# A one-core encoder layer on Trainium2: weight stores on another queue, an index row in its own buffer, merged one-hots, 48 leading u tiles

## The chip, the cores and the metric

The kernel runs on one core of a Trainium2 chip. The metric is the device time of one execution in microseconds; three executions of a kernel are timed and their median is given. A separate execution is recorded by the hardware profiler; its own time stands beside its span.

## The reference, cut to what matters

One layer on 512 tokens of width 1024 (16 meta tokens stand in front until the second half). The first half is an attention part: an input projection, differential attention and a gated linear attention in two directions, and an output projection onto the residual stream. The second half is a product-key retrieval, and it is what the change touches:

```python
q = (xi @ w_q).reshape(n, 8, 2, 128)                      # 8 heads, 2 sub-keys
s = einsum('nhpc,hpkc->nhpk', q, sub_keys)                # 128 scores each
ts, ti = top_k(s, 16)
cand_s = ts[:, :, 0, :, None] + ts[:, :, 1, None, :]      # 16 x 16 candidates
cand_i = ti[:, :, 0, :, None] * 128 + ti[:, :, 1, None, :]
best_s, best_p = top_k(cand_s, 16)
idx  = take_along_axis(cand_i, best_p)                    # 128 experts a token
gate = softmax(best_s)
act  = gelu(einsum('nd,nhkd->nhk', xi, u[idx]))
out  = einsum('nhk,nhkd->nd', gate * act, v[idx])
```

There are 128 x 128 experts, each with one row of `u` and one of `v`, 1024 wide. The sum is added to the residual stream and a last RMSNorm gives the output.

## The kernel before, in words

Tokens are taken in four tiles of 128. For tile 0 the chosen rows are gathered: 128 indirect DMAs fetch rows of `u`, VectorE makes a dot product of each with the token (L265), and 128 more fetch rows of `v`, which VectorE adds up (L263). For tiles 1 to 3, 384 tokens, the layer is computed densely: all `u` rows times all tokens, Gelu, times a matrix W of gates that is zero except at the chosen experts, times all `v` rows. All matmuls that need fp32 accuracy split each operand into a high and a low part and use three products (`mm3`, L126).

The run has these stages, with their stretches in the profile:

- 0 to about 466 us: the attention part, the projection, the 16 score units (`q` and `keys`, L919 to L940) and the searches for the 16 largest (`top16`, L182). The scores wait in a ring `sc` of SC = 16 buffers, in a pool `qs` that is closed when the searches are done.
- About 466 to 846, the middle. It interleaves two things. The u tiles, LA = 60 of them ahead of the v stage (`u_tile`, L1044): SP loads 512 KB into a ring of two buffers (`raw`, L108), ScalarE casts the high part (L114), GpSimd subtracts the low part (L116, `lo`), TensorE does 24 matmuls (L127 to L129), ScalarE applies Gelu (L1055) and stores the result to DRAM (`A_d`, L1057). And the weight building, `wbuild` (L961): the rest of the top-k (`topk2`, L189), then for each of 48 blocks of 8 tokens two one-hot tensors (L993), their products with the high and low part of the gate (L996, L994; in every fourth block ScalarE makes the high product, L999), 16 matmuls (L1021, L1022), and two copies into a staging tile (L1024). Every fourth block fills a staging tile of 2 MB, and SP stores it to DRAM (`W_d`, L1026). Four buffers hold one-hots. The first block of a token tile needs the transposed selections `sel` (L974).
- From about 846: the v stage, 128 v tiles of 18 matmuls (L1080 to L1084). It reads W and the stored activations back (L1111, L1113); the u tiles that are not leading run here, from v tile LA on, with their low part on VectorE instead of GpSimd.

How fast the building goes is set in the main loop: after u tile i, `wbuild` is advanced until the share of its cost reaches (i + 1)/(LA-ET-1), with ET = 6. The gathers are pulled by the same loops: RA a tile in the middle (from tile 12 on, L1137), RV a tile in the v stage before tile LA, RUV a tile after it (L1154). A gather is followed by its dot product when more than LAG = 3 are pending; what is left is done at the start of the v stage (`v_init`). The top-k's last tile `eq` and the gathered rows share a ring of four buffers.

The program order is not the order on the engines: a planner simulates the timeline and sets each engine's order by it. Once set, every engine and every DMA queue runs its own list in order.

SP issues all loads and the `W_d` stores from one queue; ScalarE issues the `A_d` stores. The index row 0 to 127, `iof`, is loaded by SP (L949) into a pool `wk` that takes the memory of `qs`, and VectorE spreads it into `ioh` (L950), the pattern that the one-hots compare with.

Of the kernel before, what the change touches and what calls it, by code (L numbers as in the profile page):

```python
# [9 lines left out]
F32 = mybir.dt.float32  # L10
F32R = mybir.dt.float32r
F16 = mybir.dt.float16
# [34 lines left out]
C1 = 3.0  # L47
WB = 4
WL = 1
SC = 16  # L50
TK = 1, 1, 1, 1
RB = 2
PT = {'gemm': 'g', 'half': 'g', 'meta': 'p', 'fin': 'p', 'gate': 'p', 'pair': 'a', 'kn': 'a', 'state': 'a', 'go': 'a', 'wo': 'g', 'hs': 'a', 'nat': 'a'}
# [6 lines left out]
VS = 4  # L60
VR = 5
VG = 6
RA = 0.4
RV = 0.85
RUV = 2.85
LA = 60
NCAND = 80
TCA = {'schedule_with_timeline_sim': True}
ORDER = 'GGGxGGGGGGGkGGggvgqggukugguqugguuukuvgqgukqgwuwuuuwwwuuuww'
# [13 lines left out]
def _emit(ctx, tc, I, out):  # L83
# [69 lines left out]
    hrs = cst.tile([P, NT], F32, name="hrs")  # L153
    hrow = cst.tile([P, T], F32, name="hrow")
    io16 = cst.tile([P, TOPK], F32, name="io16")

    def half(name, tag, j, n):
        return big.tile([P, KD // 2, n], F32R, name=f"{name}{j}", tag=f"{tag}{j}")
# [20 lines left out]
    def fx(name, shape, tag, dt=F32):  # L179
        return f1.tile(list(shape), dt, name=name, tag=tag)  # L180
# [8 lines left out]
    def topk2(a, b, sm, cand, tf, eq, zs):  # L189
        ts_ = tsv[:, b, 2 * a:2 * a + 2].rearrange("p t h c r -> p (t h) c r")  # L190
        ti_ = tiv[:, b, 2 * a:2 * a + 2].rearrange("p t h c r -> p (t h) c r")
        nc.vector.tensor_copy(tf, ti_)
        nc.vector.tensor_add(cand[:, :, 0:16], ts_[:, :, 1, :], ts_[:, :, 0, 0:1].to_broadcast([P, PH, 16]))
        nc.vector.tensor_add(cand[:, :, 16:72].rearrange("p h (a b) -> p h a b", b=8),
                             ts_[:, :, 1, None, 0:8].to_broadcast([P, PH, 7, 8]),
                             ts_[:, :, 0, 1:8, None].to_broadcast([P, PH, 7, 8]))
        nc.vector.tensor_add(cand[:, :, 72:80], ts_[:, :, 0, 8:16], ts_[:, :, 1, 0:1].to_broadcast([P, PH, 8]))
        bsv = sm("bsv")
        bp = sm("bp", U32)
        for h in range(PH):  # L200
            top16(bsv[:, h, :], bp[:, h, :], cand[:, h, :])
            if h % 4 == 3:
                yield
        gate = sm("gate")
        nc.vector.tensor_sub(gate, bsv, bsv[:, :, 0:1].to_broadcast([P, PH, TOPK]))
        g4 = gate.rearrange("p (t h) r -> p t (h r)", h=4)
        nc.vector.tensor_mul(g4, g4, hrs[:, 2 * a:2 * a + 2, None].to_broadcast([P, 2, 4 * TOPK]))
        def th(v):
            return v.rearrange("p (t h) r -> p t h r", h=4)

        def dst(j):
            return sel[:, j, 2 * a:2 * a + 2, 4 * b:4 * b + 4, :]

        row = sm("row", U32)
        nc.vector.tensor_scalar(row, bp, 3, None, op0=ALU.logical_shift_right)
        nc.vector.tensor_scalar(bp, bp, 7, None, op0=ALU.bitwise_and)
        rf = sm("rf")
        cf = sm("cf")
        nc.vector.tensor_copy(rf, row)
        nc.vector.tensor_copy(cf, bp)  # L220
        t9 = sm("t9")
        nc.vector.scalar_tensor_tensor(t9, rf, 9.0, cf, op0=ALU.is_equal, op1=ALU.mult)
        t1 = sm("bsv")
        nc.vector.tensor_scalar(t1, rf, 1.0, 8.0, op0=ALU.is_equal, op1=ALU.mult)
        nc.vector.tensor_add(cf, cf, t1)
        nc.vector.tensor_sub(cf, cf, t9)
        nc.vector.tensor_scalar(rf, rf, -1.0, 0.0, op0=ALU.add, op1=ALU.max)
        nc.vector.tensor_add(rf, rf, t9)
        yield
        for j, pos in enumerate((rf, cf)):  # L230
            nc.vector.tensor_tensor(eq, pos[:, :, :, None].to_broadcast([P, PH, TOPK, TOPK]),
                                    io16[:, None, None, :].to_broadcast([P, PH, TOPK, TOPK]), op=ALU.is_equal)
            nc.vector.tensor_mul(eq, eq, tf[:, :, j, None, :].to_broadcast([P, PH, TOPK, TOPK]))
            nc.vector.tensor_add(eq[:, :, :, :8], eq[:, :, :, :8], eq[:, :, :, 8:])
            nc.vector.tensor_add(eq[:, :, :, :4], eq[:, :, :, :4], eq[:, :, :, 4:8])
            nc.vector.tensor_add(eq[:, :, :, :2], eq[:, :, :, :2], eq[:, :, :, 2:4])
            nc.vector.tensor_add(dst(1 + j), th(eq[:, :, :, 0]), th(eq[:, :, :, 1]))
            if j == 0:
                yield
        nc.scalar.activation(gate, gate, AF.Exp)  # L240
        nc.vector.tensor_reduce(zs, gate, axis=AX.X, op=ALU.add)
        nc.vector.reciprocal(zs, zs)
        nc.vector.tensor_mul(dst(0), th(gate), th(zs[:, :, None].to_broadcast([P, PH, TOPK])))
        yield
# [114 lines left out]

    nc.sync.dma_start(out=ln2, in_=I["ln2"])  # L360
    nc.sync.dma_start(out=io16, in_=I["iota"][:, :TOPK].to_broadcast([P, TOPK]))
    ropc = fx("ropc", [P, TM], "ropc")
    nc.sync.dma_start(out=ropc, in_=I["ropc"])
    rops = fx("rops", [P, TM], "rops")
# [528 lines left out]
    qst = ExitStack()  # L893
    qs = qst.enter_context(tc.tile_pool(name="qs", bufs=1))

    keys = qs.tile([P, 2 * PH, NK], F32, name="keys")
    nc.sync.dma_start(out=keys, in_=I["keys"])

# [46 lines left out]
    wk = mid.enter_context(tc.tile_pool(name="wk", bufs=1))  # L945
    wk2 = mid.enter_context(tc.tile_pool(name="wk2", bufs=2))
    ioh = wk.tile([P, NK, QI], F16, name="ioh")
    iof = wk.tile([P, NK], F32, name="iof")
    nc.sync.dma_start(out=iof, in_=I["iota"].to_broadcast([P, NK]))  # L949
    nc.vector.tensor_copy(ioh, iof[:, :, None].to_broadcast([P, NK, QI]))  # L950
    sp = sparse()
    def residual(c2):
# [8 lines left out]
    def wbuild():  # L961
# [8 lines left out]
        def prep(t, m0):  # L970
            if m0 == 0:
# [2 lines left out]
                    nc.tensor.transpose(out=tr[:, j, :], in_=sel[:, j, t].rearrange("p h r -> p (h r)"), identity=ident)  # L974
                gT = wk2.tile([P, P], F32, name="gT")
                nc.scalar.activation(gT, tr[:, 0, :], AF.Copy, scale=GS)
                iT = wk2.tile([P, 2, P], F16, name="iT")
                nc.scalar.copy(iT, tr[:, 1:3, :])
                gh = wk2.tile([P, P], F16, name="gh")
                nc.vector.tensor_copy(gh, gT)  # L980
                gl = wk2.tile([P, P], F16, name="gl")
                nc.vector.tensor_sub(gl, gT, gh)
                cur[t] = gT, iT, gh, gl
            gT, iT, gh, gl = cur[t]
            sh = [P, OB // QI, NK, QI]

            def tok(v):
                return v[:, m0:m0 + OB].rearrange("p (g q) -> p g q", q=QI)[:, :, None, :].to_broadcast(sh)

            oh = big.tile([P, 4] + sh[1:], F16, name="oh", tag=("hi0", "hi1", "lo0", "lo1")[(t * P + m0) // OB % WB])  # L990
            o12, ol, od = oh[:, :2], oh[:, 2], oh[:, 3]
            for j in range(2):
                nc.vector.tensor_tensor(o12[:, j], tok(iT[:, j]), ioh[:, None, :, :].to_broadcast(sh), op=ALU.is_equal)  # L993
            nc.vector.tensor_mul(ol, o12[:, 0], tok(gl))  # L994
            if m0 // OB % DM < DN:
                nc.vector.tensor_mul(od, o12[:, 0], tok(gh))  # L996
            else:
                for m in range(OB):
                    nc.scalar.activation(od[:, m // QI, :, m % QI], o12[:, 0, m // QI, :, m % QI], AF.Copy,  # L999
                                         scale=gT[:, m0 + m:m0 + m + 1])  # L1000
# [4 lines left out]
        for n, (t, m0) in enumerate(steps):  # L1005
# [17 lines left out]
                qq = q0 + 4 * g_  # L1023
                nc.scalar.activation(stg[:, :, qq:qq + 4].rearrange("p i n -> p n i"), b, AF.Copy, scale=1.0 / GS)  # L1024
            if q0 + OB == BL:
                nc.sync.dma_start(out=W_d[:, ((t - 1) * P + m0) // BL], in_=stg)  # L1026
            yield 2.2

    U, V = {}, {}
# [238 lines left out]
```

## Time and profile before

| | before |
|---|---|
| median of three runs | 1678.32 us (1671.53 to 1680.73) |
| the profiled execution | 1682.47 us, span 1680.7 us |
| TensorE busy | 1574.4 us (94%) |
| VectorE busy | 1291.4 us (77%) |
| ScalarE busy | 739.6 us (44%) |
| GpSimd busy | 677.1 us (40%) |
| mean granted TensorE clock | 0.973 |
| moved by DMA | 387.42 MB |

The span runs from the first to the last instruction of the profiled execution. In the rows PE is TensorE, PEld its weight load, DVE VectorE, ACT ScalarE, POOL GpSimd and SP SyncE; a q behind an engine's name is its queue of DMA issues. L12 is line 12 of the kernel before. [...]

### The profile page before, as it was taken

How to read it: one execution, taken by the hardware profiler on the slowest of the kernel's cores; microseconds unless marked ns; L12 is line 12 of the kernel's file. 1: busy time of each engine (PE TensorE's matmuls, PEld its weight loads, DVE VectorE, ACT ScalarE, POOL GpSimd, SP SyncE). 2: the span in 40 equal slices, each digit the busy share in tenths (PEclk: the TensorE clock that was granted, in tenths of full speed). 3: DMA queues.
4: the chain of work that ended last, by engine and by line, in shares of the span. 5: the costliest groups of instructions: out<-in, count | busy, mean ns of one | idle time of the engine just before them, and what ended most of it. 6: DMA issues, size and time to landing. Idle time of an engine off the chain costs nothing.

```text
span 1680.7 us, 24243 instructions
## 1 busy us (share of the span) xinstructions
PE 1574.4 (94%) x8793; PEld 1392.4 (83%) x8793; DVE 1291.4 (77%) x2529; ACT 739.6 (44%) x1229; POOL 677.1 (40%) x465
## 2 busy tenths in 40 slices
PE   6999998989986789979989999999999999999998
PEld 6888886768876689878978888889999999988996
DVE  3888768647999998948247777778887888778777
ACT  5454555543324474867533333333333333333334
POOL 3443112076334467475411212154545444344442
PEclk9999999989997989999999999999999999999999
DMA  6112222232224557656999999899999998999885
GB/s 232 54 46 81 69 61 69 84 118 89 78 73 149 176 193 250 239 218 252 328 366 342 326 314 326 278 313 389 321 329 326 336 327 315 319 339 327 308 276 185
DMA packets 152360, 387.42 MB, mean 231 GB/s; under 512 B 12752, under 2 KB 71376, under 8 KB 150576
## 3 DMA queue, kind: packets, MB, share of 16 engines
q1 hardware_dynamic: 106160, 238.79, 41.2%
q0 software_dynamic: 36864, 134.23, 22.8%
q10 hardware_dynamic: 9216, 12.85, 2.1%
q8 instruction: 69, 1.13, 0.3%
q14 instruction: 51, 0.42, 0.1%
HBM read 342.56 MB, written 40.63 MB: 228 GB/s over the span
## 4 chain that ended last, share of the span: by engine, by line
PE 28%; issue 18%; DVE 12%; POOL 10%; DMA 6%; ACT 3%; SPq 1%; POOLq 0%; ACTq 0%; DVEq 0%
POOL gat L251 7%; PE banka L1080 4%; PE banka L1083 4%; PE banka L1084 4%; POOL lo L116 3%; PE bankp L1080 2%; PE bankp L1083 2%; PE bankp L1084 2%; PE bankg L129 2%; DMA gat<-v,idx 2%; PE bankg L127 2%; PE bankg L128 2%; DMA raw<-uT 2%; DVE oh L993 2%; DMA gat<-u,idx 1%
## 5 line engine op out<-in xcount | busy, mean ns | idle before, releaser
L116 POOL TENSOR_TENSOR lo<-raw,hi 128x1024 fp32r<-128x1024 f32 x81 | 238.4, 2947 | 228.8 <-ACT hi L114 220.4
L114 ACT CAST hi<-raw 128x1024 fp32r<-128x1024 f32 x177 | 185.8, 1051 | 289.6 <-PE bankg L128 159.1
L127 PE MATMUL bankg<-un_hi,hi 128*128 128x384 f32 x880 | 300.1, 341 | 12.2 <-ACT act L1055 12.2
L129 PE MATMUL bankg<-un_hi,lo 128*128 128x384 f32 x880 | 299.6, 341 | 5.3 <-POOL lo L116 5.2
L128 PE MATMUL bankg<-un_lo,hi 128*128 128x384 f32 x880 | 297.9, 338 | 0.0
L251 POOL DMA_INDIRECT gat<-u,idx x128 | 157.8, 1232 | 299.5 <-PE bankp L1084 252.1
L251 POOL DMA_INDIRECT gat<-v,idx x128 | 167.8, 1311 | 207.6 <-PE bankp L1084 180.4
L263 DVE SCALAR_TENSOR_TENSOR acc<-gat,sact,acc 128x1024 f32<-128x1024 f32 x128 | 164.2, 1283 | 72.2 <-DMA gat<-v,idx 61.6
L265 DVE CUSTOM_DVE_ANT_0 gat<-gat,hn 128x1024 f32<-128x1024 f32 x128 | 162.9, 1282 | 53.2 <-DMA gat<-u,idx 53.1
L127 PEld LDWEIGHTS bankg<-un_hi,hi 128*128 128x128 f32 x880 | 168.1, 191 | 16.1 <-ACT act L1055 12.5
L135 DVE TENSOR_TENSOR vhl<-vraw,vhl 128x1024 fp32r<-128x1024 f32 x128 | 157.1, 1228 | 30.9 <-ACT vhl L134 30.8
L129 PEld LDWEIGHTS bankg<-un_hi,lo 128*128 128x128 f32 x880 | 167.9, 191 | 8.1 <-POOL lo L116 6.8
L128 PEld LDWEIGHTS bankg<-un_lo,hi 128*128 128x128 f32 x880 | 167.7, 191 | 3.4
L134 ACT CAST vhl<-vraw 128x1024 fp32r<-128x1024 f32 x128 | 134.2, 1049 | 46.3 <-PE bankp L1084 33.4
L116 DVE TENSOR_TENSOR lo<-raw,hi 128x1024 fp32r<-128x1024 f32 x96 | 117.8, 1228 | 24.2 <-ACT hi L114 23.0
L1024 ACT ACTIVATE stg<-banka 128x512 f32<-128x512 f32 x96 | 96.2, 1140 | 1.7 <-PE banka L1022 0.9
L993 DVE TENSOR_TENSOR oh<-iT,ioh 128x1024 f16<-128x1024 f16 x96 | 80.8, 888 | 2.4 <-PE banka L1022 2.4
L1021 PE MATMUL banka<-oh 128*128 128x128 f16 x384 | 55.3, 233 | 22.1 <-DVE oh L996 12.7
L1055 ACT ACTIVATE act<-bankg 128x384 f32<-128x384 f32 x110 | 53.4, 486 | 23.2 <-PE bankg L129 12.1
L1021 PEld LDWEIGHTS <-oh 128*128 128x128 f16 x384 | 39.2, 104 | 20.8 <-DVE oh L996 15.0
L1022 PE MATMUL banka<-oh 128*128 128x128 f16 x384 | 54.3, 233 | 0.7 <-DVE oh L994 0.7
L129 PE MATMUL bankp<-un_hi,lo 128*128 128x384 f32 x144 | 48.7, 338 | 4.5 <-POOL lo L116 4.5
(2283 smaller groups left out, 3906.3 us busy)
## 6 DMA issues: line engine op xcount, KB each, us to landing
raw<-uT SPq DMA_DIRECT2D x128, 512.0 KB
vraw<-v SPq DMA_DIRECT2D x128, 512.0 KB
W_d<-stg SPq DMA_DIRECT2D x12, 2048.0 KB
wa<-W_d SPq DMA_DIRECT2D x32, 768.0 KB
A_d<-act ACTq DMA_DIRECT2D x60, 192.0 KB
wa<-A_d SPq DMA_DIRECT2D x15, 768.0 KB
raw<-wq SPq DMA_DIRECT2D x16, 512.0 KB
raw<-win_n SPq DMA_DIRECT2D x12, 512.0 KB
```

What stands on the lines that cost most here:

```text
L114: nc.scalar.copy(hi, raw)
L116: (eng or nc.vector).tensor_sub(lo, raw, hi.bitcast(F32))
L127: nc.tensor.matmul(o, lhsT=ah, rhs=bh, start=start, stop=False)
L128: nc.tensor.matmul(o, lhsT=ah, rhs=bl, start=False, stop=False)
L129: return nc.tensor.matmul(o, lhsT=al, rhs=bh, start=False, stop=stop)
L134: last[0] = nc.scalar.copy(hi, src).ins.name
L135: (eng or nc.vector).tensor_sub(lo, src, hi.bitcast(F32))
L251: g = nc.gpsimd.indirect_dma_start(out=r, out_offset=None, in_=src, in_offset=bass.IndirectOffsetOnAxis(ap=idx[:, hk:hk + 1], axis=0))
L263: nc.vector.scalar_tensor_tensor(acc0, r, sact[:, hk:hk + 1], acc0, op0=ALU.mult, op1=ALU.add)
L265: nc.vector.tensor_tensor_reduce(r, r, hn0, scale=1.0, scalar=0.0, op0=ALU.mult, op1=ALU.add, accum_out=sact[:, hk:hk + 1])
L993: nc.vector.tensor_tensor(o12[:, j], tok(iT[:, j]), ioh[:, None, :, :].to_broadcast(sh), op=ALU.is_equal)
L1080: m0 = nc.tensor.matmul(o, lhsT=gh_[:, tc_], rhs=vh[:, dc], start=(j == 0), stop=False, skip_group_check=True)
```

## The change

- `W_d` stores are issued by ScalarE instead of SP.
- `iof` moves to the pool `w1`, which stays open to the end, and its load is issued ahead of that of `keys`; SC goes from 16 to 15.
- The two one-hots of a block are made by one compare of 2048 elements instead of two of 1024, and the two products by one multiplication where VectorE makes both. For that the transposed indices `iT` and the two gate parts `gs` are laid out block by block, and the four parts of `oh` lie one after another.
- LA goes from 60 to 48; RA from 0.4 to 0.15; RUV from 2.85 to 2.7.
- The positions in the top-k are written as bf16 (`rb`, `cb`), and compared with a bf16 index row (`io16b`, one small copy at the start) instead of in fp32.

```diff
-SC = 16
+SC = 15
-RA = 0.4
+RA = 0.15
-RUV = 2.85
-LA = 60
+RUV = 2.7
+LA = 48
+    io16b = cst.tile([P, TOPK], BF, name="io16b")
+        rb = sm("rb", BF)
+        cb = sm("cb", BF)
-        nc.vector.tensor_sub(cf, cf, t9)
+        nc.vector.tensor_sub(cb, cf, t9)
-        nc.vector.tensor_add(rf, rf, t9)
+        nc.vector.tensor_add(rb, rf, t9)
-        for j, pos in enumerate((rf, cf)):
+        for j, pos in enumerate((rb, cb)):
-                                    io16[:, None, None, :].to_broadcast([P, PH, TOPK, TOPK]), op=ALU.is_equal)
+                                    io16b[:, None, None, :].to_broadcast([P, PH, TOPK, TOPK]), op=ALU.is_equal)
+    nc.vector.tensor_copy(io16b, io16)
+    iof = w1.tile([P, NK], F32, name="iof")
+    nc.sync.dma_start(out=iof, in_=I["iota"].to_broadcast([P, NK]))
     keys = qs.tile([P, 2 * PH, NK], F32, name="keys")
...
-    iof = wk.tile([P, NK], F32, name="iof")
-    nc.sync.dma_start(out=iof, in_=I["iota"].to_broadcast([P, NK]))
     nc.vector.tensor_copy(ioh, iof[:, :, None].to_broadcast([P, NK, QI]))
...
-                iT = wk2.tile([P, 2, P], F16, name="iT")
-                nc.scalar.copy(iT, tr[:, 1:3, :])
-                gh = wk2.tile([P, P], F16, name="gh")
-                nc.vector.tensor_copy(gh, gT)
-                gl = wk2.tile([P, P], F16, name="gl")
-                nc.vector.tensor_sub(gl, gT, gh)
+                iT = wk2.tile([P, P // OB, 2, OB], F16, name="iT")
+                nc.scalar.copy(iT.rearrange("p b j m -> p j b m"), tr[:, 1:3, :].rearrange("p j (b m) -> p j b m", m=OB))
+                gs = wk2.tile([P, P // OB, 2, OB], F16, name="gs")
+                g8 = gT.rearrange("p (b m) -> p b m", m=OB)
+                nc.vector.tensor_copy(gs[:, :, 0, :], g8)
+                nc.vector.tensor_sub(gs[:, :, 1, :], g8, gs[:, :, 0, :])
...
-            for j in range(2):
-                nc.vector.tensor_tensor(o12[:, j], tok(iT[:, j]), ioh[:, None, :, :].to_broadcast(sh), op=ALU.is_equal)
-            nc.vector.tensor_mul(ol, o12[:, 0], tok(gl))
-            if m0 // OB % DM < DN:
-                nc.vector.tensor_mul(od, o12[:, 0], tok(gh))
+            nc.vector.tensor_tensor(o12, tok(iT[:, blk].rearrange("p j m -> p (j m)")),
+                                    ioh[:, None, :, :].to_broadcast([P, 2 * GQ, NK, QI]), op=ALU.is_equal)
+            o12 = o12.rearrange("p (j g) k q -> p j g k q", j=2)
+            od, ol = oh[:, 2 * GQ:3 * GQ], oh[:, 3 * GQ:]
+            if blk % DM < DN:
+                nc.vector.tensor_mul(oh[:, 2 * GQ:].rearrange("p (c g) k q -> p c (g k q)", c=2).rearrange("p c (g k q) -> p c g k q", k=NK, q=QI),
+                                     o12[:, None, 0].to_broadcast([P, 2] + sh[1:]),
+                                     gs[:, blk].rearrange("p c (g q) -> p c g q", q=QI)[:, :, :, None, :].to_broadcast([P, 2] + sh[1:]))
             else:
+                nc.vector.tensor_mul(ol, o12[:, 0], tok(gs[:, blk, 1]))
...
-                nc.sync.dma_start(out=W_d[:, ((t - 1) * P + m0) // BL], in_=stg)
+                nc.scalar.dma_start(out=W_d[:, ((t - 1) * P + m0) // BL], in_=stg)
```

## Rows read from the trace of the kernel before

**Rows 1.** The stage table: busy time of each engine in five stretches, in us (with its count of instructions), then the granted clock of TensorE as a share of 2.4 GHz, the busy share of the DMA engines and GB/s.

```profile
0.00:466.00 466.00, 435.03 (x2584) 362.34 (x2584) 336.15 (x1027) 225.87 (x476) 168.81 (x151) 0.97 0.28 90
466.00:560.00 94.00, 67.64 (x358) 65.33 (x357) 91.64 (x430) 32.26 (x44) 36.58 (x16) 0.84 0.33 109
560.00:820.00 260.00, 228.44 (x1737) 218.52 (x1736) 209.32 (x239) 175.97 (x277) 157.06 (x55) 0.95 0.65 234
846.00:1092.00 246.00, 245.82 (x1094) 205.30 (x1095) 180.63 (x261) 90.25 (x126) 45.97 (x46) 0.99 0.94 324
1092.00:1640.00 548.00, 545.72 (x2760) 493.86 (x2759) 439.81 (x521) 191.56 (x262) 251.10 (x188) 1.00 0.92 325
```

**Rows 2.** TensorE's waits in the stretch 466 to 560 us: who waited for whom, us in total, times, longest.

```profile
PE bankg L127 <- ACT act L1055: 12.2, 1, 12.2
PE bankp L974 <- DVE sel L237: 8.0, 2, 5.5
PE bankp L974 <- DVE sel L243: 5.1, 1, 5.1
```

**Rows 3.** TensorE's waits in the stretch 560 to 820 us, same columns.

```profile
PE banka L1021 <- DVE oh L996: 12.7, 9, 3.4
PE banka L1021 <- ACT stg L1024: 9.3, 9, 3.7
PE bankp L129 <- POOL lo L116: 4.5, 1, 4.5
PE bankg L129 <- POOL lo L116: 4.2, 2, 3.9
```

**Rows 4.** ScalarE's groups by line in the stretch 560 to 820 us: count, then busy us and mean ns of one, then idle us ahead of them and what ended it.

```profile
L114 ACT CAST hi<-raw 128x1024 fp32r<-128x1024 f32 x40 | 42.2, 1055 | 45.2 <-DMA raw<-uT 34.6 <-PE banka L1022 5.6 <-POOL lo L116 3.2
L999 ACT ACTIVATE oh<-oh,gT 128x128 f16<-128x128 f16 x96 | 30.2, 427 | 37.2 <-DVE oh L993 37.1
L1055 ACT ACTIVATE act<-bankg 128x384 f32<-128x384 f32 x27 | 13.3, 492 | 0.0
```

**Rows 5.** VectorE's groups by line in the stretch 560 to 820 us, same columns.

```profile
L265 DVE CUSTOM_DVE_ANT_0 gat<-gat,hn 128x1024 f32<-128x1024 f32 x16 | 27.4, 1712 | 35.8 <-DMA gat<-u,idx 35.8
L231 DVE TENSOR_TENSOR eq<-sm_rf,io 128x2048 bf16<-128x2048 f32 x2 | 4.6, 2277 | 0.0
```

**Rows 6.** TensorE's order of time, the first matmul of one u tile and the first of the next, 24 matmuls later: start us, us, line, operation.

```profile
538.60 0.33 PE L127 MATMUL bankp<-un_hi,hi 128*128 128x384 f32 x1
542.75 0.33 PE L127 MATMUL bankg<-un_hi,hi 128*128 128x384 f32 x1
```

**Rows 7.** The stage table of the instructions on the one-hots `oh` alone, 560 to 820 us: PE, PEld, DVE and ACT busy us, then clock, DMA share and GB/s.

```profile
560.00:820.00 260.00, 58.20 (x768) 50.79 (x768) 149.25 (x179) 30.20 (x96) 0.95 0.65 234
```

**Rows 8.** VectorE's order of time at three places: a product of 2048 elements in bf16 and its successor; two products of 1024 in sequence; the last one-hots of an unbroken run and its successor.

```profile
583.73 1.21 DVE L233 TENSOR_TENSOR eq<-eq,tf 128x2048 bf16<-128x2048 bf16 x1
584.87 1.28 DVE L993 TENSOR_TENSOR oh<-iT,ioh 128x1024 f16<-128x1024 f16 x2
...
747.99 0.68 DVE L996 TENSOR_TENSOR oh<-oh,gh 128x1024 f16<-128x1024 f16 x1
748.60 0.68 DVE L994 TENSOR_TENSOR oh<-oh,gl 128x1024 f16<-128x1024 f16 x1
...
751.61 1.28 DVE L993 TENSOR_TENSOR oh<-iT,ioh 128x1024 f16<-128x1024 f16 x2
760.47 2.84 DVE L265 CUSTOM_DVE_ANT_0 gat<-gat,hn 128x1024 f32<-128x1024 f32 x1 [7.58 <-DMA gat<-u,idx]
```

**Rows 9.** ScalarE's order of time around the issue of one activation's store: start us, us, and in brackets the idle time ahead and what ended it.

```profile
516.10 0.33 ACTq L1057 DMA_DIRECT2D A_d<-act  x1
516.54 1.04 ACT L114 CAST hi<-raw 128x1024 fp32r<-128x1024 f32 x1 [0.47 <-ACT act L1055]
```

**Rows 10.** The waits of SP's DMA queue in the stretch 440 to 850 us: who waited for whom, us in total, times, longest.

```profile
SPq L1026 <- ACT stg L1024: 26.0, 10, 8.2
SPq L949 <- DVE tiv L187: 21.3, 1, 21.3
```

**Rows 11.** The waits that the index row and the loads behind it caused, stretch 462 to 546 us, same columns.

```profile
ACT hi L114 <- DMA raw<-uT: 21.8, 1, 21.8
DVE ioh L950 <- DMA iof<-iota: 2.2, 1, 2.2
```

**Rows 12.** SP's issues around one weight store, in order of time: start us, us, line, transfer; x2 is a merged row of two issues, the first at its start.

```profile
718.32 3.85 SPq L108 DMA_DIRECT2D raw<-uT  x2
725.27 0.33 SPq L1026 DMA_DIRECT2D W_d<-stg  x1
725.70 7.68 SPq L108 DMA_DIRECT2D raw<-uT  x2
```

**Rows 13.** ScalarE's casts that waited for two of these loads, in order of time.

```profile
721.98 1.05 ACT L114 CAST hi<-raw 128x1024 fp32r<-128x1024 f32 x1 [5.35 <-DMA raw<-uT]
736.29 1.05 ACT L114 CAST hi<-raw 128x1024 fp32r<-128x1024 f32 x1 [3.16 <-DMA raw<-uT]
```

**Rows 14.** GpSimd's order of time: two low parts.

```profile
742.60 12.51 POOL L116 TENSOR_TENSOR lo<-raw,hi 128x1024 fp32r<-128x1024 f32 x1 [2.64 <-ACT hi L114]
756.23 2.37 POOL L116 TENSOR_TENSOR lo<-raw,hi 128x1024 fp32r<-128x1024 f32 x1
```

More of the change, by code (lines that the diff above doesn't have):

```diff
@@ L976, in prep @@
                 nc.scalar.activation(gT, tr[:, 0, :], AF.Copy, scale=GS)
-                iT = wk2.tile([P, 2, P], F16, name="iT")
-                nc.scalar.copy(iT, tr[:, 1:3, :])
-                gh = wk2.tile([P, P], F16, name="gh")
-                nc.vector.tensor_copy(gh, gT)
-                gl = wk2.tile([P, P], F16, name="gl")
-                nc.vector.tensor_sub(gl, gT, gh)
-                cur[t] = gT, iT, gh, gl
-            gT, iT, gh, gl = cur[t]
-            sh = [P, OB // QI, NK, QI]
@@ L987, in tok @@
-            def tok(v):
-                return v[:, m0:m0 + OB].rearrange("p (g q) -> p g q", q=QI)[:, :, None, :].to_broadcast(sh)
-            oh = big.tile([P, 4] + sh[1:], F16, name="oh", tag=("hi0", "hi1", "lo0", "lo1")[(t * P + m0) // OB % WB])
-            o12, ol, od = oh[:, :2], oh[:, 2], oh[:, 3]
-            for j in range(2):
-                nc.vector.tensor_tensor(o12[:, j], tok(iT[:, j]), ioh[:, None, :, :].to_broadcast(sh), op=ALU.is_equal)
-            nc.vector.tensor_mul(ol, o12[:, 0], tok(gl))
@@ new lines, in prep @@
+                cur[t] = gT, iT, gs
+            gT, iT, gs = cur[t]
+            GQ = OB // QI
+            sh = [P, GQ, NK, QI]
+            def tok(v):
+                n = v.shape[1] // QI
+                return v.rearrange("p (g q) -> p g q", q=QI)[:, :, None, :].to_broadcast([P, n, NK, QI])
+            oh = big.tile([P, 4 * GQ, NK, QI], F16, name="oh", tag=("hi0", "hi1", "lo0", "lo1")[(t * P + m0) // OB % WB])
+            o12 = oh[:, :2 * GQ]
+            blk = m0 // OB
+            nc.vector.tensor_tensor(o12, tok(iT[:, blk].rearrange("p j m -> p (j m)")),
+                                    ioh[:, None, :, :].to_broadcast([P, 2 * GQ, NK, QI]), op=ALU.is_equal)
```

## The prediction

> **What bounds the kernel now.** I read the stage table first, then the waits of each engine inside the stages that are not full, then the groups by line, and last the time order around single waits. In the stage table [rows 1] the reader is to see two kinds of stage. From 846 us on TensorE is busy in 246 of 246 us and 546 of 548, at a granted clock of 0.99 and 1.00: the v stage is bound by TensorE, whatever the others do. The middle, 466 to 846, is where time is lost: TensorE is busy 67.6 of 94 us (clock 0.84), then 228.4 of 260 (0.95). [...] So I treat TensorE's matmuls as a fixed amount of work and ask how much idle and slow clock the change takes out of the middle, and what it puts back in the v stage.
>
> In 466:560 VectorE is full (91.6 of 94): its top-k chain sets the end. TensorE waits there once for 12.2 us and three times for the selections, 13.1 us [rows 2]. In 560:820, the weight building, TensorE (228), VectorE (209) and ScalarE (176) all have much to do. TensorE's 30.7 us of waits [rows 3] go to the one-hots (12.7), to the staging copies that free a bank (9.3) and to GpSimd's low parts (8.7). Behind these stand ScalarE's waits of 34.6 us for u tiles to land and 37.1 for one-hots [rows 4], and VectorE's 35.8 us for gathered rows [rows 5].
>
> **The leading u tiles, 60 to 48.** Twelve tiles go from the middle into the last stage. A tile is 24 matmuls, 538.60 to 542.75, so 4.15 us at full clock [rows 6]. The v stage is full, so it pays all of them: 12 x 4.15 = **+50**. It has cover for what comes with them: twelve more low parts on VectorE, and the dot products that leave the middle, some 30 us spread over a stage in which VectorE now idles 108 of 548 us [rows 1]. Without that cover the price is those 30 us. The pulls still end with the last tile (4 + 37 + 216 = 257 for 256 gathers). Twelve activation stores and three reloads fewer are worth nothing: TensorE is the bound where they run.
>
> **The building stretch.** The pace loop spreads the weight building over LA-ET-1 tiles, 41 now instead of 53. I make the new load of each engine in what was 560:820.
> TensorE: the weight matmuls take 58.2 us [rows 7]; the other 170.2 are 40 u tiles (the count of casts [rows 4]), 4.25 each. Of the 40, twelve leave; three more should run earlier, in the 12.2 us hole (next part). 58.2 + 25 x 4.25 = 164.
> VectorE: the sixteen dot products (27.4 us) leave [rows 5], since 4 pulls are all that 30 x 0.15 gives and the lag of 3 keeps even these until the stage's end. The one-hots and products, 179 instructions, are 149 us busy [rows 7], yet undisturbed ones start 0.60 us apart [rows 8], which makes 108; the other 41 us are stretching beside GpSimd's 40 low parts, 1.0 each. Twelve to fifteen low parts fewer give back some 13. 209.3 - 27.4 - 13 - 5 (merging, below) = 164.
> ScalarE: fifteen casts and activations fewer, 15 x 1.54 = 23 [rows 4], and twelve issues more, which cost their 0.33 us and a wait of 0.47 as the issue of an activation's store does [rows 9], 10 us: 176 - 23 + 10 = 163.
> So all three come to about 164. The stretch now exceeds its fullest engine by 260 - 228 = 32 us. Bounds for that excess: down to 12, if only TensorE's 8.7 us for low parts and a few more are left; up to 62, twice as much, since three equal loads in fixed orders wait for one another more. I keep 32: the waits for gathers and landings go, the even loads bring others. 164 + 32 = 196 instead of 260: **-64**.
>
> **The index row.** Its load sits in SP's queue until the last score tile is free: SP waits 21.3 us [rows 10], and queued behind it are the u loads, so ScalarE stands 21.8 us at a cast [rows 11] and the activation, low part and matmuls behind it are late. In its own buffer it is loaded early; the wait goes. What is late next is VectorE: it waited only 2.2 us for the row [rows 11] and is full all along. So the stretch 466:560 itself gains 2.2, perhaps as much again where low parts slide beside searches that they don't stretch: **-4**, bounds 0 and -12. The real gain is the three tiles above. The ring of 15 score tiles costs nothing: the sixteenth would reuse a tile whose searches ended long before; at worst it delays one score copy, for one unit of four searches, some 5 us.
>
> **Weight stores on ScalarE's queue.** SP stood 26.0 us in ten waits for staging copies [rows 10], with u loads behind. On ScalarE the store follows its own copy; queued behind it there are only casts and copies, which it holds for the 0.8 us counted above; TensorE waits for those copies, and that is in the load of ScalarE. A u load issued just behind a 2 MB store, at 725.70, reached its cast at 736.29, one issued at 718.32 already at 721.98 [rows 12, 13]. [...] By the row the load stands behind the store by about 7 us. ScalarE's wait there was 3.2 us, as the load is asked for some time ahead; if each of twelve stores cost that, it would be all the 34.6 us of landings, so I bound the part by 0 and 35 us of ScalarE's waiting. What reaches TensorE of it is inside the excess of 32, so it gets no term of its own.
>
> **Merged one-hots.** 48 pairs of compares and 36 of products become one of 2048. The nearest row is a 2048 product in bf16, 1.14 us to the next start against 2 x 0.60 [rows 8]: 84 x 0.06 = 5 us, used above. If the new pattern lost the packed rate, each would cost as an unpacked 2048 compare, 2.28 [rows 5], 84 x 1.1 = 92 us more on VectorE; the innermost pair is as it was, so I leave that out of the sum.
>
> **The bf16 compare in the top-k.** Eight compares take 2.28 us each undisturbed [rows 5]; at the packed rate of the 2048 product they would take 1.21 and give 8 x 1.07 = 8.6 us. But the position is one element repeated along the innermost axis. I take 0 and keep -4 (the half that lies ahead of 560) in the range, within the -12. [...]
>
> The extra copy of sixteen indices at the start is one small instruction in a stage where VectorE is busy 336 of 466 us [rows 1]: 0, and at worst its own length, which is below the 0.60 us of a 1024-wide one-hot.
>
> **Sum.** +50 - 64 - 4 = -18. The profiled execution took 1682.47 (span 1680.7): 1664.5. The runs' median is 1678.32, 4.2 lower, so I forecast **1660 us**. From no change a measurement of this kernel can tell about 0.5%, 8.4 us.
>
> **Rivals.**
> GpSimd starves (slower). A low part that takes 2.4 us took 12.51 while VectorE ran one-hots and products without a gap until 752.9 [rows 8, 14]; TensorE then waited 4.5 [rows 3]. Dot products that waited for their rows left such gaps; they are gone and merged operations leave half as many. If each of the twelve store groups held one low part until the four one-hot buffers were full, eight more waits of 4.2 us: excess 66, stretch 230, sum +16, **1694**. It decides from about four such waits beyond my sum. Against: fifteen low parts fewer, and the two long waits of now cost TensorE 8.4. Chance 0.14.
> The stall only moves. TensorE reaches the transposes of the selections in a fixed order; if these stay behind the same tiles, the 12.2 us come back there, nothing slides, and with an excess up to 40 the stretch is 177 + 32 to 40: sum -5 to +3, **1676**. For it: VectorE is full before 560. Against: the transposes stand inside u tiles, so the planner sets them by its own clock, and it will see the early loads. Chance 0.20.
> The excess shrinks to 12, as its causes were the gather waits and late landings: stretch 176, with -8 ahead of it: -42, **1636**. For it: 35.8 us of VectorE's idle go. Against: three even loads. Chance 0.22.
> My forecast, excess 22 to 42: -28 to -8, 1650 to 1670: chance 0.44.
>
> The range: the fast rival to the slow one, less the outer ends: 1634 to 1690. Faster by over 0.5%: 0.44 + 0.22 = 0.66; within: 0.20; slower: 0.14.
>
> **What would show it.** No cast waiting 20 us for a u load near 490, and more u tiles done when the building starts; the weight building done in about 196 us; u loads issued without waits for staging copies; merged products at 1.14 to 1.2 us; the compare still 2.28; the v stage 50 us longer for its 12 tiles. I am wrong if low parts over 6 us multiply, if TensorE's waits for one-hots pass 25 us, or if the v stage is no longer full.

## The result, and the profile after

The change made the kernel slower: 1698.6 us median beside 1678.5 of the kernel before, ratio 1.0124 (95% interval 1.0081 to 1.0166). A second measurement of the same two kernels gave 1691.6 beside 1679.1, 1.0076 (1.0052 to 1.0100). So it lost 13 to 20 us where 18 were forecast as a gain. The profiled execution took 1698.0, span 1695.9.

The stage table of the changed kernel, cut at events: the first u tile's first matmul (469.70), the first weight matmul (579.90), the last staging copy (775.00), the first v matmul (805.20). Columns as in [rows 1].

```profile
469.70:579.90 110.20, 77.12 (x421) 75.71 (x422) 109.96 (x441) 36.94 (x55) 42.55 (x16) 0.88 0.31 104
579.90:775.00 195.10, 164.23 (x1374) 155.59 (x1374) 149.28 (x118) 152.47 (x239) 99.53 (x30) 0.93 0.61 223
775.00:805.20 30.20, 21.05 (x121) 20.41 (x119) 4.80 (x7) 7.92 (x13) 7.33 (x4) 0.90 0.98 345
805.20:1695.90 890.70, 877.68 (x4296) 776.74 (x4296) 675.16 (x866) 313.69 (x449) 323.47 (x253) 1.00 0.88 309
```

The same cuts in the trace of the kernel before:

```profile
466.20:566.70 100.50, 73.27 (x388) 70.88 (x389) 98.14 (x436) 33.25 (x47) 40.51 (x17) 0.85 0.35 116
566.70:816.70 250.00, 219.36 (x1684) 209.66 (x1684) 202.62 (x231) 173.66 (x271) 152.48 (x53) 0.95 0.65 232
816.70:846.20 29.50, 22.58 (x132) 22.26 (x130) 5.29 (x7) 8.00 (x13) 7.81 (x4) 0.96 1.04 370
846.20:1680.60 834.40, 824.05 (x4008) 727.28 (x4008) 648.97 (x830) 298.65 (x425) 307.46 (x241) 0.99 0.91 318
```

The v stage grew by 56.3 us. The weight building shrank by 54.9. The stretch ahead of it, from the first u tile to the first weight matmul, grew by 9.7, and VectorE is full in it in both kernels. The rest of the 15 us stands in front (466.2 to 469.7), and that is not the change's: a second profile of the changed kernel began its u tiles at 462.9. Single profiles of one program differ by some us a stage, so I take each size below from timed runs or from sums over long stretches.

TensorE's waits of the changed kernel ahead of the building, and then in it:

```profile
PE bankp L978 <- DVE sel L246: 21.6, 1, 21.6
PE bankp L978 <- DVE sel L240: 4.6, 1, 4.6
...
PE bankp L127 <- ACT act L1066: 2.8, 1, 2.8
```

```profile
PE banka L1032 <- DVE oh L1004: 18.7, 7, 8.3
PE bankg L129 <- POOL lo L116: 11.2, 2, 8.2
PE banka L1032 <- ACT stg L1035: 3.1, 5, 1.8
```

The 12.2 us for a u tile [rows 2] are gone, but the wait of the first transpose of a selection grew from 5.1 to 21.6: 17.3 us together before, 21.6 now. With the later waits for selections it is 25.3 and 26.2. This first transpose, before and after:

```profile
517.65 0.48 PE L974 MATMUL bankp<-ident,sel 128*128 128x128 f32 x1 [5.13 <-DVE sel L243]
```

```profile
521.74 0.47 PE L978 MATMUL bankp<-ident,sel 128*128 128x128 f32 x1 [21.61 <-DVE sel L246]
```

It starts 51.4 us after the first u tile in the kernel before and 52.0 in the changed one, so the earlier index row brought TensorE no further. In the building the waits for staging copies fell (9.3 [rows 3] to 3.1), and those for one-hots rose from 12.7 to 18.7.

### The profile page after: what moved, and what is told of

Read it like the earlier page. It is cut to its first block, busy times and chain, and to the rows that moved or that the text cites. A ratio compares the mean times of both kernels' runs of the same rounds, so it can differ in the third digit from the quotient of the medians.

```text
span 1695.9 us, 24079 instructions
## 1 busy us (share of the span) xinstructions
PE 1581.4 (93%) x8793; PEld 1394.1 (82%) x8793; DVE 1275.4 (75%) x2458; ACT 736.8 (43%) x1229; POOL 646.2 (38%) x453
## 4 chain that ended last, share of the span: by engine, by line
issue 25%; PE 19%; DVE 13%; POOL 11%; DMA 6%; ACT 3%; SPq 1%; POOLq 0%; ACTq 0%; DVEq 0%
POOL gat L254 10%; DMA gat<-u,idx 3%; PE banka L1091 2%; PE banka L1095 2%; PE banka L1094 2%; DVE oh L999 2%; DMA gat<-v,idx 1%; PE bankg L129 1%; PE bankg L128 1%; PE bankg L127 1%; ACT stg L1035 1%; POOL lo L116 1%; PE bankp L1091 1%; PE bankp L1094 1%; PE bankp L1095 1%
## 5 line engine op out<-in xcount | busy, mean ns | idle before, releaser
L129 PE MATMUL bankg<-un_hi,lo 128*128 128x384 f32 x912 | 309.1, 339 | 11.9 <-POOL lo L116 11.9
L127 PE MATMUL bankg<-un_hi,hi 128*128 128x384 f32 x912 | 309.2, 339 | 0.0
L128 PE MATMUL bankg<-un_lo,hi 128*128 128x384 f32 x912 | 308.7, 338 | 0.0
L116 POOL TENSOR_TENSOR lo<-raw,hi 128x1024 fp32r<-128x1024 f32 x69 | 201.9, 2928 | 251.2 <-ACT hi L114 242.8
L268 DVE CUSTOM_DVE_ANT_0 gat<-gat,hn 128x1024 f32<-128x1024 f32 x128 | 156.0, 1223 | 70.9 <-DMA gat<-u,idx 70.2
L128 PEld LDWEIGHTS bankg<-un_lo,hi 128*128 128x128 f32 x912 | 173.3, 190 | 3.4
L116 DVE TENSOR_TENSOR lo<-raw,hi 128x1024 fp32r<-128x1024 f32 x108 | 132.5, 1227 | 13.4 <-ACT hi L114 12.5
L999 DVE TENSOR_TENSOR oh<-iT,ioh 128x2048 f16<-128x2048 f16 x48 | 76.6, 1627 | 9.6 <-PE banka L1033 9.5
L1032 PE MATMUL banka<-oh 128*128 128x128 f16 x384 | 52.0, 225 | 23.8 <-DVE oh L1004 18.7
L1004 DVE TENSOR_TENSOR oh<-oh,gs 128x2048 f16<-128x2048 f16 x36 | 53.4, 1512 | 0.1
L1033 PE MATMUL banka<-oh 128*128 128x128 f16 x384 | 51.6, 224 | 0.0
```

Of the source, the lines that this page charges most:

```text
L116: (eng or nc.vector).tensor_sub(lo, raw, hi.bitcast(F32))
L127: nc.tensor.matmul(o, lhsT=ah, rhs=bh, start=start, stop=False)
L128: nc.tensor.matmul(o, lhsT=ah, rhs=bl, start=False, stop=False)
L129: return nc.tensor.matmul(o, lhsT=al, rhs=bh, start=False, stop=stop)
L268: nc.vector.tensor_tensor_reduce(r, r, hn0, scale=1.0, scalar=0.0, op0=ALU.mult, op1=ALU.add, accum_out=sact[:, hk:hk + 1])
L999: nc.vector.tensor_tensor(o12, tok(iT[:, blk].rearrange("p j m -> p (j m)")), ioh[:, None, :, :].to_broadcast([P, 2 * GQ, NK, QI]), op=ALU ...
```

## The experiments

All ratios are to the kernel before, run on the same chip; over the chips its median was 1678.7 to 1680.2 us.

**Code and numbers apart.** Four kernels make a square: code of before or after, numbers (LA, RA, RUV) of before or after.

```diff
# e1: the code after, the numbers before
-RA = 0.15
+RA = 0.4
-RUV = 2.7
+RUV = 2.85
-LA = 48
+LA = 60
```

> The changed kernel's code (early index row, stores on ScalarE, merged one-hots, bf16 compare) with the numbers of before: 60 leading u tiles, RA 0.4, RUV 2.85. Theory 'the numbers': the loss comes with moving 12 u tiles and the dot products into the last stage; the code alone then stands at 1670 to 1682 us, and the last stage is 834 us long as before. Rival 'the code': the edits cost the 15 to 20 us; then 1690 to 1700, with the last stage back at 834 and the middle longer than before by 15 or more.

Measured: 1668.7, ratio 0.9942 (0.9913 to 0.9971): 11 us **faster** than before. The mirror image, e2, is the code of before with 48 tiles, RA 0.15 and RUV 2.7:

> The kernel before with 48 leading u tiles, RA 0.15, RUV 2.7 and nothing else. 'The numbers': 1692 to 1705, as the changed kernel. 'The code': 1672 to 1684. If the two parts only help together (the edits pay for what the numbers cost), it is slower than the changed kernel: above 1705.

Measured: 1707.0, 1.0170 (1.0112 to 1.0227). The code gained; the numbers lost 27 us with the old code and 23 with the new. The loss is the numbers' alone. (1707.0 lies a little above both ranges: the code gains 11 us at 60 tiles and 15 at 48, which the intervals don't tell apart.) From the first u tile to the first v matmul ("the middle") the four took 380.0 and 366.5 us (60 tiles, old and new code), 348.6 and 335.5 (48 tiles). The code shortens it by 13 either way, and twelve tiles and the dot products that left shorten it by only 31, while the v stage, from its first matmul to TensorE's last, pays 51 to 58.

**The index row.** For scale, the changed kernel was run again:

> The changed kernel itself, once more, as the measure for its variants on the same chip. 1690 to 1702 us; its first matmul of the weight building again some 110 us after the first u tile begins.

It is the 1691.6 above. With the row loaded where it was, in the pool that takes the score tiles' memory (e4):

```diff
-    iof = w1.tile([P, NK], F32, name="iof")
...
+    iof = wk.tile([P, NK], F32, name="iof")
     nc.sync.dma_start(out=iof, in_=I["iota"].to_broadcast([P, NK]))
```

> The changed kernel with the index row loaded where it was, behind the score tiles; the order of instructions on every engine is otherwise the same. 'The stall only moves' (VectorE's top-k chain sets when TensorE goes on): same time within 4 us of the changed kernel, 1695 to 1703, TensorE's wait for a u tile of some 12 us returns and its first wait for the selection falls from 21.6 to about 8, the two together 20 to 22 as now. Rival 'the row was worth its wait': 8 to 14 us slower than the changed kernel.

Measured: 1690.3, 1.0075 (1.0046 to 1.0105), no difference. TensorE's waits ahead of its building:

```profile
PE bankg L127 <- ACT act L1066: 16.3, 1, 16.3
PE bankg L129 <- POOL lo L116: 13.0, 2, 11.9
PE bankp L978 <- DVE sel L240: 7.7, 2, 4.8
...
PE bankp L978 <- DVE sel L246: 0.2, 1, 0.2
```

The hole is back, 16.3 us, and the first transpose waits 0.2 for its selection and starts 51.5 us after the first u tile. One wait covers the other; the selections from VectorE set the end of both. The 13.0 us for low parts came later in the same stretch, which was 10 us longer than the changed kernel's; the whole middle took 330.2 us, beside 331.1 in the changed kernel's second profile.

**The stores on SP again (e5).**

```diff
-                nc.scalar.dma_start(out=W_d[:, ...], in_=stg)
+                nc.sync.dma_start(out=W_d[:, ...], in_=stg)
```

> The changed kernel with the twelve weight stores issued by SP again. If ScalarE's issues keep the copies and casts behind them waiting (a cost of the change): 3 to 10 us faster than the changed kernel. If they free SP's queue as meant: 3 to 15 us slower, with SP waiting some 20 us for staging copies and ScalarE's casts waiting longer for u tiles. If hidden either way: within 3 us of the changed kernel.

Measured: 1688.5, 1.0068 (1.0043 to 1.0093), beside 1.0076: hidden either way, though SP stands 43.6 us in eleven waits again:

```profile
SPq L1037 <- ACT stg L1035: 43.6, 11, 12.1
```

**What stands ahead of the first one-hots.** In the changed kernel the planner puts five compares of the top-k on VectorE ahead of the first weight matmul, in e1 three: part of the third selection, which only the next token tile needs, has moved in front. I held it back (e10):

```diff
+        r_ = nc.vector.tensor_scalar(row, bp, 3, None, ...)
+        if held:
+            tc.add_manual_dep(r_.ins, held[1], ORDER_DEP, reason="hold")
```

Here `held` lists the products of the one-hots, so the decoding of a late selection follows the second group.

> The changed kernel with one ordering added: on VectorE the decoding and compares of the third selection (needed only by the second third of the weights) stay behind the second group of one-hots. In the kernel before two compares of it's kind stood ahead of the first one-hots less; with 48 tiles the planner puts the third selection's there. Theory 'a late selection stands ahead of the first one-hots': the time from the first u tile to the first weight matmul falls from 110 to about 97 us, and the time by 6 to 14 us, to 1680 to 1690. Rival 'the tiles are merely moved, the order doesn't matter' (what VectorE does first it needn't do later): that time falls as well, but the building grows by as much; total within 4 us of the changed kernel.

Measured: 1689.2, 1.0061 (1.0045 to 1.0078), the same as the changed kernel. The time to the first weight matmul fell from 109.7 (its second profile) to 86.6, and the building grew from 190.5 to 209.7:

```profile
469.10:555.70 86.60, 60.17 (x333) 58.76 (x334) 85.53 (x343) 27.51 (x40) 33.24 (x13) 0.86 0.32 104
555.70:765.40 209.70, 180.27 (x1463) 171.01 (x1463) 189.62 (x216) 162.64 (x254) 104.74 (x33) 0.95 0.60 220
```

VectorE's work moved from one stretch to the other, and its time with it. This reason, the first I had, fell: the order is not the cause, the amount of work may be.

**Tiles and dot products apart.** The changed code with 60 tiles and RA 0.15 (RUV 2.99), e6:

> The changed kernel's code with 60 leading u tiles, but few dot products in the middle (RA 0.15; RUV 2.99 so that all are still pulled). Tells the tiles from the dot products. If the loss comes from pushing the dot products into the last stage: 1678 to 1695. If it comes from the twelve tiles: as the same code with RA 0.4, 1664 to 1673. My forecast that VectorE gains by losing them in the middle would make it 3 to 10 us faster than that: 1658 to 1666.

Measured: **1656.8**, 0.9874 (0.9842 to 0.9905), 22 us faster than before and the fastest kernel of this study. So sending the dot products out of the middle gains 12 us on e1, a little more than the 3 to 10 expected, and the v stage takes them without growing (first v matmul to TensorE's last: 824.6 us, 824.9 in e1). The tiles lose: from here to the changed kernel it is 35 us for twelve. (LA also sets the pace of the building; no run separates the two.) The count between and beyond:

> The changed kernel's code with 52 leading u tiles, RA 0.25, RUV 2.73. If the loss grows with every tile moved (8 of 12): 1683 to 1692. If most of it is the third selection's place on VectorE, which the planner's order shows at 52 no longer all ahead of the first one-hots: 1672 to 1681.

> The changed kernel's code with 64 leading u tiles, RA 0.15, RUV 3.12: the other way from the change. So far a tile moved out of the last stage saves it 4.75 us and costs the middle 2.1 to 2.4. If that still holds: 1644 to 1650. If the middle at 60 is bound by TensorE already (209 of 229 us busy in the building), a tile costs there what it saves: 1653 to 1660.

> 68 leading u tiles, RA 0.15, RV 0.95, RUV 3.15. As before: 1632 to 1642 if a tile still costs the middle half of what it saves, 1652 to 1664 if the middle is full, or more dot products a tile hold up the last stage.

Measured: 52 tiles 1687.0 (1.0046, 1.0022 to 1.0071), 64 tiles 1664.1 (0.9905, 0.9876 to 0.9934), 68 tiles 1667.8 (0.9934, 0.9915 to 0.9953). 64 and 68 tiles are slower than either of their forecasts; only for 68 is the loss against 60 clear of the intervals. The middle and the rest of the span in the profiles, one row of the stage table each, for 48 (the second profile), 52, 60, 64 and 68 tiles:

```profile
462.90:794.00 331.10, 263.17 (x1913) 252.22 (x1913) 271.08 (x564) 197.40 (x305) 143.22 (x49) 0.91 0.55 198
794.00:1682.00 888.00, 875.56 (x4296) 776.82 (x4296) 675.92 (x866) 314.22 (x449) 320.28 (x253) 1.00 0.88 310
```

```profile
467.20:805.40 338.20, 277.37 (x2009) 266.05 (x2009) 283.03 (x573) 203.26 (x313) 157.84 (x57) 0.93 0.59 209
805.40:1677.50 872.10, 859.14 (x4200) 760.73 (x4200) 667.08 (x854) 309.37 (x441) 313.42 (x249) 1.00 0.88 312
```

```profile
464.10:821.50 357.40, 303.45 (x2201) 294.05 (x2202) 296.73 (x569) 216.20 (x329) 169.39 (x63) 0.95 0.60 211
821.50:1653.70 832.20, 823.31 (x4008) 727.63 (x4008) 658.46 (x850) 299.83 (x425) 323.13 (x251) 0.99 0.91 324
```

```profile
467.60:838.20 370.60, 323.88 (x2297) 314.37 (x2297) 296.46 (x569) 221.84 (x337) 182.57 (x67) 0.94 0.60 211
838.20:1660.20 822.00, 805.96 (x3912) 710.66 (x3912) 656.81 (x846) 291.35 (x417) 333.90 (x251) 0.99 0.92 327
```

```profile
468.40:857.60 389.20, 340.75 (x2393) 331.94 (x2393) 293.09 (x570) 227.60 (x345) 201.97 (x72) 0.95 0.60 211
857.60:1667.60 810.00, 790.12 (x3816) 694.64 (x3816) 651.47 (x840) 286.08 (x410) 311.44 (x250) 0.99 0.93 329
```

The price of one tile in the middle is no constant: 2.2 us from 48 to 60 tiles ((357.4 - 331.1) / 12), 4.0 from 60 to 68 ((389.2 - 357.4) / 8). Only the second is about what a stage charges that TensorE bounds [rows 6]. The steps between are too small for single profiles: the two of the changed kernel differ by 4.4 us in the middle, and the kernel with 52 tiles has more dot products there (RA 0.25). Beyond 60 the rest of the span also gives back less, 2.8 us a tile ((832.2 - 810.0) / 8) where a tile had cost it 4.65 below, as TensorE's unused time in it grows from 8.9 to 19.9 us. Of the five counts 60 is the best. As tiles leave the middle, TensorE's unused time there rises (54 us of 357 at 60 tiles, 68 of 331 at 48) and its clock falls (0.95 to 0.91).

**Is it VectorE?** The merged products are left out, so VectorE has less to do and the other engines have the same instructions:

```diff
-                nc.vector.tensor_mul(oh[:, 2 * GQ:] ...)
+                od = ol = o12[:, 0]
```

> The changed kernel (48 tiles) without the 36 merged products on VectorE: the weight matmuls read the one-hots of the second index in their place, so three quarters of the weights are without their gates, and the rest is as it was. That is some 43 us of VectorE's work less in the middle, with TensorE's, ScalarE's and the DMAs' the same. If VectorE's work holds TensorE up in the middle at 48 tiles, the time falls by 20 to 40 us, to 1652 to 1672. If the losses come from the fixed order among the engines (TensorE for ScalarE's copies, low parts, transposes), by less than 12.

> The same omission at 60 leading tiles (RA 0.15, RUV 2.99), whose kernel with all its products took 1657. If twelve more u tiles give TensorE work to do while VectorE is late, VectorE matters less here: 4 to 15 us faster, 1642 to 1653, less than half of what the omission gives at 48. If the omission gives as much here as there, the number of tiles has nothing to do with what VectorE costs.

Measured: at 48 tiles (e11) 1668.0 (0.9925, 0.9898 to 0.9951), 24 us less than the changed kernel. At 60 tiles (e12) 1649.9 (0.9818, 0.9774 to 0.9861), 7 us less than with the products (9 by the ratios), an interval that still overlaps. The middle of the two:

```profile
465.00:773.70 308.70, 255.64 (x1913) 245.89 (x1913) 213.72 (x528) 196.94 (x305) 121.21 (x49) 0.93 0.60 213
```

```profile
468.30:815.70 347.40, 307.20 (x2202) 298.19 (x2202) 231.10 (x533) 215.41 (x329) 158.47 (x63) 0.95 0.61 217
```

At 48 tiles 57 us less of VectorE's busy time shorten the middle by 22 (331.1 to 308.7), at 60 tiles 66 us by 10. The omission shortens GpSimd's time too, so I compare TensorE's waits in the middle for one-hots and low parts: the changed kernel (second profile), the same without products, and 60 tiles with products:

```profile
PE banka L1032 <- DVE oh L1004: 19.3, 7, 6.5
...
PE bankg L129 <- POOL lo L116: 4.1, 2, 3.3
...
PE banka L1033 <- DVE oh L1008: 2.7, 1, 2.7
```

```profile
PE banka L1030 <- DVE oh L999: 6.6, 3, 4.5
...
PE bankg L129 <- POOL lo L116: 0.8, 1, 0.8
```

```profile
PE banka L1032 <- DVE oh L1004: 5.8, 5, 2.0
PE bankp L129 <- POOL lo L116: 1.5, 1, 1.5
PE bankg L129 <- POOL lo L116: 0.4, 1, 0.4
```

At 48 tiles the omission takes 15.4 us of waits for one-hots (22.0 to 6.6) and 3.3 of waits for low parts, so most of what it gives comes from VectorE itself; and with 60 tiles TensorE waited only 5.8 us for one-hots to begin with. With fewer tiles in it the middle depends more on VectorE, and so less on TensorE.

**Where the code's gain comes from.** Each part alone undone, or the dots alone moved, at 60 tiles and RA 0.15, beside the 1656.8 of all parts:

> The kernel before with RA 0.15 and RUV 2.99 in place of 0.4 and 2.85, and nothing else: the dot products leave the middle, the tiles stay. If dots and edits gain separately: 1666 to 1672 (the dots gained 12 with the edits in). If the dots gain only where the edits have taken other waits away: within 4 us of the kernel before.

> All code edits, 60 tiles, RA 0.15, with the weight stores issued by SP again. If the stores' queue makes part of the edits' gain: 1660 to 1668. If it gives nothing, as at 48 tiles: 1653 to 1660.

> All code edits, 60 tiles, RA 0.15, with the one-hots and products as they were, 1024 elements each. My sum had 5 us of VectorE for the merge; VectorE's work counts by a quarter at 60 tiles (7 us for 43), so 1 to 3 us: 1656 to 1661. If the merge is most of the edits' gain: 1663 to 1670.

> All code edits, 60 tiles, RA 0.15, with the index row loaded behind the score tiles again. If the selections hold TensorE up anyway, as at 48 tiles: 1655 to 1661. If the late row is most of the edits' gain: 1663 to 1670.

Measured: old code (e16) 1675.9 (0.9985, 0.9965 to 1.0006), stores on SP (e17) 1660.3 (0.9893, 0.9875 to 0.9911), one-hots unmerged (e18) 1671.9 (0.9960, 0.9940 to 0.9980), row back (e19) 1661.3 (0.9894, 0.9876 to 0.9913). Stores and row give 3 to 5 us, with intervals that overlap that of all parts. The merge gives 15 beside the kernel of all parts and 11 to 12 beside the other two, which are merged too: more than either forecast. With the old code the dots' leaving gives 3 us, within the measurement. The profiles show less of a contrast: the merge shortens the middle by 8.9 (366.3 to 357.4), and the dots' leaving shortens it by 9.1 with the new code and by 9.8 with the old (380.0 to 370.2). It is not VectorE's work: that is 292.4 us of the middle unmerged and 296.7 merged. The building of both, unmerged first:

```profile
566.90:806.20 239.30, 217.41 (x1689) 208.87 (x1688) 189.87 (x206) 172.25 (x264) 139.74 (x46) 0.96 0.63 227
```

```profile
562.00:790.70 228.70, 209.32 (x1683) 201.53 (x1683) 194.18 (x130) 172.84 (x266) 120.20 (x46) 0.99 0.66 237
```

GpSimd's column is 139.7 unmerged and 120.2 merged, half of the difference in its six gather issues (18.3 and 8.8 us). TensorE's waits for its low parts are 7.4 and 1.9 us (0.7 and 1.8 in the other two merged kernels):

```profile
PE bankp L129 <- POOL lo L116: 5.1, 1, 5.1
...
PE bankg L129 <- POOL lo L116: 2.3, 1, 2.3
```

```profile
PE bankp L129 <- POOL lo L116: 1.5, 1, 1.5
PE bankg L129 <- POOL lo L116: 0.4, 1, 0.4
```

For nearly the same matmuls TensorE is busy 8 us less, at 0.99 instead of 0.96. That low parts come in time more often beside merged instructions would fit the waits, which are 5.5 us of the 15; no run showed it by itself. What makes up the rest, and why the timed runs give the dots a gain only together with the merge, stays open.

## Why the prediction was wrong, point by point

**The tiles' return: the step that failed.** I took TensorE's matmuls as the bound of the middle, so that a tile that left gave back 4.25 us there and cost 4.15 later, about zero, and the three tiles that were to slide came on top. Measured from 60 to 48 tiles: 2.2 us a tile back ((357.4 - 331.1) / 12) and 4.65 paid ((888.0 - 832.2) / 12), so 29 us lost by the profiles and 35 by the runs; the kernels with stores on SP and with the row back lose 28 and 29 over the same step (e17 to e5, e19 to e4). The forecast's own rows had VectorE full ahead of 560 and at 209 of 260 us after; I subtracted its 45 us of relief and still let TensorE set the time, plus a fixed 32. But at 48 tiles that excess was in good part VectorE's doing: 57 us less of its work take 22 from the middle (e11). VectorE's busy time in the middle fell by 42.0 us (306.1 to 264.0), about the 45 of the forecast, and the middle by 44.5 instead of 68. Part of a tile's price seems to be that it lengthens VectorE's work: from 48 to 60 tiles that grows from 271.1 to 296.7 us with 564 and 569 instructions, from 60 to 68 not at all. That this is the 2.2 us a tile was not tested. The forecast's signs of being wrong did not warn of it: the waits for one-hots rose to 18.7 us, not past 25, and the v stage stayed full (877.7 of 890.7).

**The building in 196 us** came out at 195.1, with an excess of 30.9, by luck: between these events it had taken 250.0 before, not 260, so it fell by 54.9 and not by 64. I had three tiles slide into a hole for nothing. 1.4 more tiles did run ahead of the building (17.1 instead of 15.7 in TensorE's order), but the stretch ahead grew by 9.7 instead of shrinking by 4. e10 shows that the cut between the two stretches means little; the middle as a whole is what counts: forecast -68, measured -44.5 (-48.9 by the second profile).

**The index row.** "The stall only moves" is what happened, the rival to which I gave 0.20 (though not its time, 1676), and that the early row gains nothing is shown by e4. My argument against it, that the planner would see the early load, was beside the point: TensorE's order hardly changed (the first transposes stand after 7.0 tiles, 7.2 before), and they wait for VectorE, busy 110.0 of 110.2 us there.

**The dot products** gained as forecast in direction, 12 us with the changed code and 3, within the measurement, with the old.

**The v stage.** 53.6 us more by TensorE's busy time (824.1 to 877.7), 56.3 by the stretch, where I had 50. Its clean groups of eight v tiles with eight u tiles take 66.5 us against 34.9 without, 3.95 a tile, a little under the forecast's 4.15; in the changed kernel the first such groups take between 66.5 and 68.2 us, with waits of at most 1.4 us for `gh_` between. Why they come with 48 tiles I did not settle.

**Stores, row buffer, bf16.** No term for the stores: right (e5, e17). My 0 for the compares in bf16 was a choice, made because the position is one element repeated along the innermost axis; that this decides their time was not shown. The time bore the 0 out: where nothing disturbs them they take 2.28 us each, 2278 ns the one below, 2277 those with fp32 positions [rows 5]:

```profile
L234 DVE TENSOR_TENSOR eq<-sm_rb,io16b 128x2048 bf16<-128x2048 bf16 x1 | 2.3, 2278 | 0.0
```

**The merge** was sized at 5 us of VectorE and hidden in the excess; it is worth 11 to 15 at 60 tiles, not through VectorE's own time. One merged product and one merged compare where no low part runs beside them:

```profile
604.03 1.21 DVE L1004 TENSOR_TENSOR oh<-oh,gs 128x2048 f16<-128x2048 f16 x1
605.17 1.21 DVE L999 TENSOR_TENSOR oh<-iT,ioh 128x2048 f16<-128x2048 f16 x1
```

They take the 1.21 us of the 2048 product in [rows 8], and not the 2.28 of the compare in [rows 5], so the 92 us that I left out of the sum did not come. What sets these two rates no run separated. I had even named the merge as a danger to GpSimd ("leave half as many" gaps). Long low parts did occur, 12.8 us at 579.90:

```profile
579.90 12.84 POOL L116 TENSOR_TENSOR lo<-raw,hi 128x1024 fp32r<-128x1024 f32 x1 [8.25 <-DVE oh L1004]
...
594.09 2.39 POOL L116 TENSOR_TENSOR lo<-raw,hi 128x1024 fp32r<-128x1024 f32 x1
```

But TensorE waited 11.2 us for low parts where it had waited 8.7, so this rival explains at most 2.5 us (in the second profile they are 4.1); the time came out at its 1694 by another way.

The sum made anew, by timed runs: tiles +34.8 (1656.8 to 1691.6), dots -11.8 (1668.7 to 1656.8), code -11.5 (1680.2 to 1668.7) = +11.5; measured in the second comparison, +12.5. The three are steps along one path from the kernel before to the changed one, so that they add up is no test of them.

## What to carry to other kernels

Before moving work from one stage to another, ask of each stage what a unit of it costs there, not how long it takes: a tile of 4.15 us cost 2.2 us in the stage where TensorE waited for another engine, and 4.65 in the stage that TensorE bounded. Work that fills another engine's waits is the cheapest in the kernel, and the share of a change that is only numbers can outweigh three good edits. When a wait disappears in front of a full engine, look for the next wait behind the same engine before counting it.

## What the runs showed of the hardware

In the building of the last comparison GpSimd's 40 low parts took 127.4 us beside VectorE's instructions of 1024 elements and 118.2 beside those of 2048, the first row and the second:

```profile
L116 POOL TENSOR_TENSOR lo<-raw,hi 128x1024 fp32r<-128x1024 f32 x40 | 127.4, 3190 | 98.0 <-ACT hi L114 95.6 <-PE banka L1026 2.2
```

```profile
L116 POOL TENSOR_TENSOR lo<-raw,hi 128x1024 fp32r<-128x1024 f32 x40 | 118.2, 2960 | 105.3 <-ACT hi L114 99.5 <-PE bankg L129 5.7
```

That the merge shortens low parts is not shown by this: the other two merged kernels of that comparison took 125.1 (e17) and 125.3 us (e19) for 40. The other direction is plain in the kernel before, from 466 to 820 us: VectorE's products of 1024 elements took 0.68 us each where no low part ran beside them and 1.2 on average where one did, while its searches (0.2 to 0.3 us) took the same either way.

In the kernel before, the granted clock stood at 0.50 in TensorE's longest idle of [rows 2], 12.16 us, and in the 14 us from 508 on; from 524 to 528 it was 1.00:

```profile
500.00:508.00 8.00, 0.00 (x0) 0.00 (x0) 5.64 (x43) 0.66 (x1) 0.00 (x0) 0.50 0.44 140
508.00:522.00 14.00, 7.01 (x20) 6.00 (x21) 14.00 (x93) 6.51 (x9) 7.07 (x3) 0.50 0.41 131
524.00:528.00 4.00, 4.00 (x25) 4.00 (x25) 4.00 (x13) 2.08 (x3) 2.39 (x1) 1.00 0.18 55
```

Matmuls of 384 columns started 0.32 us apart in the second of these stretches and 0.17 in the third:

```profile
508.82 0.69 PE L127 MATMUL bankg<-un_hi,hi 128*128 128x384 f32 x1 [12.16 <-ACT act L1055]
...
518.56 0.52 PE L129 MATMUL bankg<-un_hi,lo 128*128 128x384 f32 x1
518.88 0.52 PE L127 MATMUL bankg<-un_hi,hi 128*128 128x384 f32 x1
...
524.16 0.33 PE L129 MATMUL bankp<-un_hi,lo 128*128 128x384 f32 x1
524.34 0.33 PE L127 MATMUL bankp<-un_hi,hi 128*128 128x384 f32 x1
```

This is the slow clock of the prediction. The trace gives the clock as a share of full speed alone, 0.50 or 1.00; the frequency that [rows 1] names stands in no view.
